# Four residual tiles and branch B's values, transposed as the rounded 32-bit type

## The chip, the core and the metric

One core of a Trainium2 chip runs the whole kernel. The time is device microseconds of one execution; the median of three runs is given. TensorE multiplies and also transposes 128x128 tiles (a matmul in transpose mode, with an identity matrix as second operand); VectorE and ScalarE do elementwise work; GpSimd (POOL) does small elementwise work and issues DMAs on its own queue; SyncE (SP) issues most of the other DMAs.

## The reference, cut to what matters

```
h = x + 1/2 * SwiGLU_1(RMSNorm(x))
u = RMSNorm(h)
[qA|kA|vA|qB|kB|vB|gA|gB] = u @ W_in
yA = NeighbourhoodAttention2D(qA, kA, vA)          # learned 2-D bias
yB = WindowedGQA(rope(qB), rope(kB), vB)           # learned sink logit
h = h + (sigmoid(gA) * (yA @ W_A) + sigmoid(gB) * (yB @ W_B)) @ W_out
h = h + 1/2 * SwiGLU_2(RMSNorm(h))
y = RMSNorm_final(h)
```

1024 tokens, width 1024, hidden width 2816, all in 32-bit floats.

## The kernel before

**Matmuls.** Every large product is done in three terms: an operand is split into a high part of the rounded 32-bit type (`F32R`) and a low part (`split`: ScalarE rounds to the high part, VectorE subtracts), and `mm3` issues high x high (L149), high x low (L153) and low x high (L155). Large products go through a Strassen scheme of seven products, P1 to P7, over 2x2 blocks (`products`); they need the blocks B11 and B21, made of the first four token tiles, and B22, T1, T2, T3 and T4, which also need the last four.

**Change of stage.** Between two parts of the layer the residual stream lies with tokens on the partitions, in eight tiles of 128 tokens (`res(t)`, tiles 0 to 3 in `fx`, 4 to 7 in `fa`); the next product needs it transposed. There are two such changes: from the first FFN to the input projection (`down1`, about 578 to 670 us), and from the attention's output to the second FFN (`down2`, about 1244 to 1296 us). `transition` runs them as a generator: for each tile, `pre` finishes it; `normed` squares it on ScalarE (L127), makes the factor on POOL (L130, L131) and scales it on VectorE into a buffer of the tag `xs` (L133); `turn_tile`, here `to_strassen`, transposes it with `turned` (8 transposes of 128x128 into two PSUM banks of the tag `d`, L142) and makes the Strassen blocks from the banks; `post` then drains ten steps of the early products, which fill TensorE between two tiles. The tag `xs` has two buffers, so tile t+1 is scaled while tile t waits to be turned. In the first change the tiles come in two halves of four. While tiles 4 to 7 go through, the top right block is kept in DRAM (`u_d`); for the last tile its copy is staged in the `xs` buffer that the tile itself lay in.

**Branch B's values.** `v_b` loads them (128 x 1024) from DRAM into an `xs` buffer, and `turn_v` transposes them with eight transposes (L1163).

**Order.** The first stage has an order written out by hand. In everything behind it a planner orders each engine's instructions at build time: it takes them in program order as priority, assumes a duration for each, and issues whichever is ready by its reckoning. Buffers of a tag are handed on when their last reader is done. `pin` keeps an instruction behind the one traced before it on its engine.

Other users of the identity `ident` are the warm-up transposes (`keep_busy`, L919), the spreading of statistics (L986) and the attention's probabilities (L1620).

The function `turned` is all of the transposing:

Of the kernel before, what the change touches and what calls it, by code (L numbers as in the profile page):

```python
# [9 lines left out]

F32 = mybir.dt.float32
# [20 lines left out]
def f32v(ap):  # L32
    return ap.bitcast(F32)
# [3 lines left out]
def trunk_kernel(ctx, tc, x, xt, n1, wg1, wu1, wd1, nm, win, rpb, sink, wa, wb, wout,  # L37
# [16 lines left out]
    def nm_(s):  # L54
        uid[0] += 1
        return f"{s}_{uid[0]}"

    ident = const.tile([P, P], F32, name="ident")
    make_identity(nc, ident)
    nhalf4 = const.tile([P, 4], F32, name="nhalf")  # L60
    nc.gpsimd.memset(nhalf4, -0.5)
    nhalf = nhalf4[:, 0:1]
# [72 lines left out]
        return xs  # L135

    def turned(xs):
        pts = []
        for half in range(2):
            pt = bank("d")  # L140
            for c in range(4):
                nc.tensor.transpose(pt[:, c * P:(c + 1) * P], xs[:, (half * 4 + c) * P:(half * 4 + c + 1) * P], ident)  # L142
            pts.append(pt.rearrange("p (c t) -> p c t", c=4))
        return pts

# [18 lines left out]

        return fx[t] if t < 4 else fa[:, (t - 4) * 1024:(t - 3) * 1024]

    def transition(pre, gain, turn_tile, post, halves=1, ahead=2):

        h, xs = {}, {}
        n = NTT // halves  # L170
        for base in range(0, NTT, n):
            for t in (base, base + 1):
                h[t] = pre(t)
            xs[base] = normed(h.pop(base), gain)
            yield
            for t in range(base, base + n):
                for k in range(t + 2, t + 1 + ahead) if base and t == base else (t + (ahead if base else 2),):
                    if k < base + n:
                        h[k] = pre(k)
                if t + 1 < base + n:  # L180
                    xs[t + 1] = normed(h.pop(t + 1), gain)
                turn_tile(t, xs.pop(t))
                if t:
                    post(t - 1)
                yield
        post(NTT - 1)
# [6 lines left out]

    kept = []

    def to_strassen(t, xs):

        pa, pb = turned(xs)
        tt = t % 4
        cols = slice(tt * P, (tt + 1) * P)  # L200

        def put(o, src, eng=None):
            h, l = rhs(o)
            split(h[:, :, cols], l[:, :, cols], src, eng)

        x11 = res(tt)[:, :512].rearrange("p (c t) -> p c t", c=4)
        x21 = res(tt)[:, 512:].rearrange("p (c t) -> p c t", c=4)
        if t < 4:
            put(B11, pa)
            put(B21, pb)  # L210
            nc.scalar.copy(x11, pa)
            nc.scalar.copy(x21, pb)
            return
        t1 = res(t)[:, :512].rearrange("p (c t) -> p c t", c=4)
        t2 = res(t)[:, 512:].rearrange("p (c t) -> p c t", c=4)
        nc.vector.tensor_tensor(t1, pa, x11, op=ALU.subtract)
        put(T1, t1)
        nc.vector.tensor_tensor(t2, pb, t1, op=ALU.subtract)
        put(T2, t2)
        put(B22, pb)  # L220
        nc.vector.tensor_tensor(x11, t2, x11, op=ALU.subtract)
        nc.vector.tensor_tensor(x21, x21, t2, op=ALU.subtract)
        if kept:
            x12 = xs[:, :512] if t == NTT - 1 else main.tile([P, 512], F32, tag="s1", bufs=1, name=nm_("s1"))
            nc.scalar.copy(x12.rearrange("p (c t) -> p c t", c=4), pa)
            nc.sync.dma_start(kept[0][t - 4], x12)

# [686 lines left out]
    def keep_busy(n):  # L914

        b = bank("g")
        for i in range(n):
            k = i % 4 * P
            nc.tensor.transpose(b[:, k:k + P], ident, ident)  # L919

    def first_stage():
        load, _, _, _, pieces, (multiply, finish), hand_over, load_early = hg
# [39 lines left out]
        def do(op, a):  # L962
# [3 lines left out]
            elif op == "add":  # L966
                d, e = [sq[k] for k in sums[int(a[0])]]
                nc.vector.tensor_tensor(d, d, e, op=ALU.add)
            elif op == "sum":
                i = int(a[0])  # L970
                if i == 0:
                    mean.append(bank("g"))
                for k in range(4):
                    nc.tensor.matmul(mean[0][:, k * P:(k + 1) * P], sq[3 * i][:, k * P:(k + 1) * P], ones, start=i + k == 0, stop=i == 1,
                                     skip_group_check=True)
            elif op == "eps":
                i = int(a[0])
                nc.vector.tensor_scalar(st[i][1], st[1][0] if i else mean[0].rearrange("p (k c) -> p k c", c=P)[:, :, 0], EPS, None, op0=ALU.add)
            elif op == "pow":
                i = int(a[0])  # L980
                nc.gpsimd.tensor_tensor(st[i][0], st[i][1], nhalf4, op=ALU.pow)
            elif op == "spread":
                i = int(a[0])
                r[i] = bank("d" if i else "g")
                for k in range(4):
                    nc.tensor.transpose(r[i][:, k * P:(k + 1) * P], st[i][0][:, k:k + 1].to_broadcast([P, P]), ident)  # L986
            elif op == "stat":
                t = int(a[0])
                nc.scalar.activation(toks[:, t - 4], toks[:, t - 4], AF.Square, scale=D ** -0.5,
                                     accum_out=st[1][0][:, t - 4:t - 3])  # L990
            elif op == "keep":
                rms["row"] = main.tile([P, 512], F32, tag="s1", bufs=1, name=nm_("s1"))
                nc.scalar.copy(rms["row"], r[0])
            elif a[0] == "X":
                c = int(a[1])
                h, l = [v[:, c, :] for v in rhs(B21)]
                if op == "hi":
                    nc.scalar.activation(h, block(c, 0, 1), AF.Copy, scale=n1c[:, 4 + c:5 + c])
                else:
                    nc.vector.scalar_tensor_tensor(out=l, in0=block(c, 0, 1), scalar=n1c[:, 4 + c:5 + c], in1=f32v(h),  # L1000
                                                   op0=ALU.mult, op1=ALU.subtract)
            elif op == "y":
                n, h, c = int(a[0][0]) - 1, int(a[0][1]) - 1, int(a[1])
                d, k = block(c, h, n), 4 * n + c
                nc.vector.scalar_tensor_tensor(out=d, in0=d, scalar=n1c[:, k:k + 1],
                                               in1=rms["row"] if (n, h) == (1, 0) else r[h], op0=ALU.mult, op1=ALU.mult)
            elif op == "t":
                c = int(a[1])
                y11, y21, y12, y22 = block(c, 0, 0), block(c, 0, 1), block(c, 1, 0), block(c, 1, 1)
                d, u, v = {"1": (y12, y12, y11), "2": (y22, y22, y12), "3": (y11, y22, y11), "4": (y21, y21, y22)}[a[0]]  # L1010
                nc.vector.tensor_tensor(d, u, v, op=ALU.subtract)
            elif a[0] in RIGHTS:
                c = int(a[1])
                src, g = block(c, *BLOCKS[a[0]]), RIGHTS[a[0]]
                if ar[g].dtype != F32R:
                    new_ar(g)
                h, l = [v[:, c, :] for v in rhs(RIGHTS[a[0]])]
                if op == "hi":
                    nc.scalar.copy(h, src)
                else:  # L1020
                    nc.vector.tensor_tensor(l, src, f32v(h), op=ALU.subtract)
            elif op == "load":
                i, m, half = [int(k) for k in a]
                load(i, m, half, {(0, 0): 4, (0, 1): 5, (1, 0): 6}[m, half])
            else:
                q = int(a[1]), a[0], int(a[2])
                if op == "mm":
                    if q not in mm:
                        mm[q] = multiply(*q)
                    drain(mm[q], 1)  # L1030
                elif op == "x":
                    drain(finish(*q), 1)
                else:
                    if q not in pc:
                        pc[q] = pieces(*q)
                    pc[q].pop(op)()
# [115 lines left out]

    def v_b():
        mix["vb"] = [new_fx(k, F32R).rearrange("p (t d) -> p t d", t=NTT) for k in (0, 1)]
        mix["vr"] = xs4()
        pin(nc.sync.dma_start(mix["vr"], z_d[17 * P:18 * P, :]))

    def turn_v():
        r = mix["vr"]
        for n in range(2):  # L1160
            pt = bank("g")
            for i in range(4):
                nc.tensor.transpose(pt[:, i * P:(i + 1) * P], r[:, (4 * n + i) * P:(4 * n + i + 1) * P], ident)  # L1163
            pt = pt.rearrange("p (b s d) -> p b s d", s=2, d=HD)
            for s in range(2):
                v = mix["vb"][s][:, 4 * n:4 * n + 4, :]
# [447 lines left out]
    def turn(un):  # L1614
        nk = un["nk"]
        un["p"] = [ws4()[:, :768].rearrange("p (k s t) -> p k s t", k=3, s=2) for _ in range(2)]
        for s in range(2):
            pt = bank("d")
            for i in range(nk):
                nc.tensor.transpose(pt[:, i * P:(i + 1) * P], un["pr"][s][:, i * P:(i + 1) * P], ident)  # L1620
            if len(un["v"]) == 2:
                dst = [un["p"][s][:, :nk, k, :] for k in range(2)]
            else:
# [317 lines left out]
```

## Time and profile before

| | |
|---|---|
| median of 3 runs | 1912.23 us (1911.99 to 1912.38) |
| the profiled execution | 1912.05 us, span of the profile 1910.1 us |
| instructions | 26150, of these 9020 matmuls or transposes |
| TensorE's granted clock, mean | 0.999 |
| DMA over the span | 192 GB/s |

The span runs from the first to the last instruction. An engine's busy time is the union of its instructions; matmuls overlap one another, so a row's duration is longer than the distance to the next start, and it is this distance that a matmul costs. PEld is TensorE's loading of weights, which overlaps. A transpose is shown as a MATMUL that reads `ident`. The type "f32" is shown for plain and rounded 32-bit operands of TensorE alike.

### The profile page before, as it was taken

The numbers are of one execution on the slowest core, as the hardware profiler recorded it, in microseconds if no ns is written. First come the engines' busy times: TensorE is split into PE (matmuls) and PEld (weight loads), VectorE is DVE, ScalarE is ACT, GpSimd is POOL, SyncE is SP. The second block draws the span as 40 slices with busy tenths as digits, with TensorE's granted clock in tenths as the row PEclk, the third lists the DMA queues.
The fourth block names the chain that finished last, engine by engine and source line by source line (L and its number), as shares of the span: only waits on it lengthen the run. The fifth ranks groups of instructions, "written<-read, shape, count | busy, mean of one in ns | idle before, by whom it ended". The sixth has DMA issues, their size and how long they took to land.

```text
span 1910.1 us, 26150 instructions
## 1 busy us (share of the span) xinstructions
PE 1901.1 (100%) x9020; PEld 1595.1 (84%) x9020; DVE 1456.1 (76%) x2644; ACT 961.3 (50%) x1876; POOL 244.3 (13%) x453
## 2 busy tenths in 40 slices
PE   9999999999999999999999999999999999999998
PEld 8888888888888888898898888888888888888886
DVE  8988888868957788666888999789665566559664
ACT  7533545544446543444898885274333333344453
POOL 0011232210000112211112300010010001000011
PEclk9999999999999999999999999999999999999999
DMA  7256977887454367855647969653333323492341
GB/s 270 95 188 217 336 273 289 298 293 282 127 166 135 112 206 225 243 192 206 181 123 207 296 227 335 232 195 132 136 111 107 108 89 111 162 357 93 110 139 61
DMA packets 176963, 365.84 MB, mean 192 GB/s; under 512 B 17728, under 2 KB 75968, under 8 KB 176832
## 3 DMA queue, kind: packets, MB, share of 16 engines
q1 hardware_dynamic: 136784, 236.23, 37.6%
q0 software_dynamic: 39184, 126.90, 19.2%
q8 instruction: 71, 1.16, 0.3%
q10 hardware_dynamic: 864, 1.05, 0.2%
q14 instruction: 60, 0.49, 0.1%
HBM read 244.06 MB, written 121.83 MB: 192 GB/s over the span
## 4 chain that ended last, share of the span: by engine, by line
PE 96%; ACT 2%; DVE 1%; DMA 0%; issue 0%; SPq 0%; POOLq 0%; POOL 0%; DVEq 0%
PE g L149 18%; PE g L155 18%; PE g L153 18%; PE d L155 12%; PE d L149 12%; PE d L153 12%; PE d L1620 2%; PE g L1634 1%; PE d L1596 1%; PE d L1597 1%; PE g L1639 1%; PE d L142 1%; ACT fa L1604 0%; ACT ws L95 0%; DMA fx<-in_xt_dram 0%; DVE ws L98 0%
## 5 line engine op out<-in xcount | busy, mean ns | idle before, releaser
L149 PE MATMUL g<-ar,ws 128*128 128x512 f32 x1062 | 407.0, 393 | 0.2
L153 PE MATMUL g<-ar,ws 128*128 128x512 f32 x1062 | 403.8, 390 | 0.0
L155 PE MATMUL g<-ar,ws 128*128 128x512 f32 x1062 | 402.6, 390 | 0.0
L149 PE MATMUL d<-ar,ws 128*128 128x512 f32 x706 | 275.3, 390 | 0.0
L155 PE MATMUL d<-ar,ws 128*128 128x512 f32 x706 | 274.9, 389 | 0.1
L153 PE MATMUL d<-ar,ws 128*128 128x512 f32 x706 | 274.8, 389 | 0.0
L155 PEld LDWEIGHTS g<-ar,ws 128*128 128x128 f32 x1062 | 199.2, 188 | 41.8
L153 PEld LDWEIGHTS g<-ar,ws 128*128 128x128 f32 x1062 | 199.4, 188 | 40.7
L149 PEld LDWEIGHTS g<-ar,ws 128*128 128x128 f32 x1062 | 196.4, 188 | 37.1 <-ACT xs L1331 1.1
L334 DVE TENSOR_TENSOR ws<-raw,ws 128x512 fp32r<-128x512 f32 x216 | 147.6, 689 | 78.5 <-ACT ws L327 77.7
L327 ACT CAST ws<-raw 128x512 fp32r<-128x512 f32 x216 | 132.7, 620 | 143.1 <-PE g L155 61.2
L155 PEld LDWEIGHTS d<-ar,ws 128*128 128x128 f32 x706 | 132.5, 188 | 28.0 <-DVE ws L334 0.5
L153 PEld LDWEIGHTS d<-ar,ws 128*128 128x128 f32 x706 | 132.6, 188 | 27.7 <-DVE ar L1000 0.3
L149 PEld LDWEIGHTS d<-ar,ws 128*128 128x128 f32 x706 | 132.7, 188 | 27.1
L95 ACT CAST ws<-raw 128x512 fp32r<-128x512 f32 x88 | 54.9, 623 | 115.5 <-PE d L155 63.6
L98 DVE TENSOR_TENSOR ws<-raw,ws 128x512 fp32r<-128x512 f32 x88 | 60.5, 688 | 55.2 <-ACT ws L95 55.1
L95 ACT CAST ar<-raw 128x512 fp32r<-128x512 f32 (+1 forms) x80 | 52.1, 654 | 84.4 <-PE g L153 51.5
L446 POOL DMA_DIRECT2D hid<-fx x91 | 49.5, 544 | 343.2 <-DVE fx L506 221.6
L149 PE MATMUL g<-ws,ws 128*128 128x512 f32 x232 | 90.9, 392 | 0.0
L153 PE MATMUL g<-ws,ws 128*128 128x512 f32 x232 | 90.3, 389 | 0.0
L155 PE MATMUL g<-ws,ws 128*128 128x512 f32 x232 | 90.1, 390 | 0.0
L95 ACT CAST ws<-ar 128x512 fp32r<-128x512 f32 x104 | 64.3, 618 | 47.4 <-PE g L155 25.4
(382 smaller groups left out, 3878.7 us busy)
## 6 DMA issues: line engine op xcount, KB each, us to landing
raw<-hid SPq DMA_DIRECT2D x70, 512.0 KB
hid<-fx POOLq DMA_DIRECT2D x91, 256.0 KB, 2.9
ar<-in_ffn_w_down_dram SPq DMA_DIRECT2D x32, 512.0 KB
raw<-in_ffn_w_up_dram SPq DMA_DIRECT2D x31, 512.0 KB
wo_d<-made POOLq DMA_DIRECT2D x28, 512.0 KB, 4.6
raw<-in_ffn_w_gate_dram SPq DMA_DIRECT2D x27, 512.0 KB
hid<-fa POOLq DMA_DIRECT2D x51, 256.0 KB, 2.9
ar<-zs_d POOLq DMA_DIRECT2D x48, 256.0 KB, 9.3
```

The lines of the kernel that those rows point to most:

```text
L95: hi = nc.scalar.copy(dst_hi, src)
L98: (eng or nc.vector).tensor_tensor(dst_lo, src, f32v(dst_hi), op=ALU.subtract)
L142: nc.tensor.transpose(pt[:, c * P:(c + 1) * P], xs[:, (half * 4 + c) * P:(half * 4 + c + 1) * P], ident)
L149: o = nc.tensor.matmul(b, lhs[0], r[0], start=first, stop=False, **kw)
L153: nc.tensor.matmul(b, lhs[0], r[1], start=False, stop=False, **kw)
L155: nc.tensor.matmul(b, lhs[1], r[0], start=False, stop=last, **kw)
L327: nc.scalar.copy(w[0][:, :512], a)
L334: nc.vector.tensor_tensor(w[0][:, 512:], a, f32v(w[0][:, :512]), op=ALU.subtract)
L446: nc.gpsimd.dma_start(hid[PRODUCTS.index(p), i], src)
L1596: nc.tensor.matmul(b[:, :nw], un["q"][s], un["kd"][s][:, k0 * P:k1 * P], start=True, stop=False)
L1597: nc.tensor.matmul(b[:, :nw], un["q"][s], un["kl"][s][:, k0 * P:k1 * P], start=False, stop=True)
L1620: nc.tensor.transpose(pt[:, i * P:(i + 1) * P], un["pr"][s][:, i * P:(i + 1) * P], ident)
```

## The change

The identity is made as a tile of the rounded type, and every other user reads it through a view as plain 32-bit float (`f32v`). In `transition`, for the tiles in `moved` (5 and 7, counted from 0, so the sixth and the eighth), the scaled tile is moved by a DMA on POOL's queue (512 KB, SBUF to SBUF, pinned in program order) into a second buffer of the tag `xs`, which has the rounded type; `turned` transposes that one with both operands and the result viewed as the rounded type. The bits are moved as they are. For the last tile of the first change of stage the staging of the top right block uses the buffer before the move (`spare`). Branch B's values are loaded into a tile declared with the rounded type and transposed as that type; the load is the same.

```
-    ident = const.tile([P, P], F32, name="ident")
-    make_identity(nc, ident)
+    ident = const.tile([P, P], F32R, name="ident")
+    nc.gpsimd.memset(f32v(ident), 0.0)
+    nc.gpsimd.affine_select(out=ident, in_=f32v(ident), compare_op=ALU.not_equal, fill=1.0, base=0, pattern=[[-1, P]],
+                            channel_multiplier=1)
...
     def turned(xs):
-        pts = []
+        i, pts = f32v(ident) if xs.dtype == F32 else ident, []
...
-                nc.tensor.transpose(pt[:, c * P:(c + 1) * P], xs[:, (half * 4 + c) * P:(half * 4 + c + 1) * P], ident)
+                nc.tensor.transpose(pt[:, c * P:(c + 1) * P].bitcast(xs.dtype), xs[:, (half * 4 + c) * P:(half * 4 + c + 1) * P], i)
...
-    def transition(pre, gain, turn_tile, post, halves=1, ahead=2):
+    def transition(pre, gain, turn_tile, post, halves=1, ahead=2, moved=(5, 7)):
...
+        def norm(t):
+            x = y = normed(h.pop(t), gain)
+            if t in moved:
+                x = main.tile([P, 1024], F32R, tag="xs", bufs=2, name=nm_("moved"))
+                pin(nc.gpsimd.dma_start(f32v(x), y))
+            xs[t] = x, y
...
-            xs[base] = normed(h.pop(base), gain)
+            norm(base)
...
-                    xs[t + 1] = normed(h.pop(t + 1), gain)
-                turn_tile(t, xs.pop(t))
+                    norm(t + 1)
+                turn_tile(t, *xs.pop(t))
...
-    def to_strassen(t, xs):
+    def to_strassen(t, xs, spare):
...
-            x12 = xs[:, :512] if t == NTT - 1 else main.tile([P, 512], F32, tag="s1", bufs=1, name=nm_("s1"))
+            x12 = spare[:, :512] if t == NTT - 1 else main.tile([P, 512], F32, tag="s1", bufs=1, name=nm_("s1"))
...
-        mix["vr"] = xs4()
-        pin(nc.sync.dma_start(mix["vr"], z_d[17 * P:18 * P, :]))
+        mix["vr"] = main.tile([P, 1024], F32R, tag="xs", bufs=2, name=nm_("vr"))
+        pin(nc.sync.dma_start(f32v(mix["vr"]), z_d[17 * P:18 * P, :]))
...
-                nc.tensor.transpose(pt[:, i * P:(i + 1) * P], r[:, (4 * n + i) * P:(4 * n + i + 1) * P], ident)
+                nc.tensor.transpose(pt[:, i * P:(i + 1) * P].bitcast(F32R), r[:, (4 * n + i) * P:(4 * n + i + 1) * P], ident)
```

The other lines of the diff replace `ident` by `f32v(ident)` where plain 32-bit data is transposed.

More of the change, by code (lines that the diff above doesn't have):

```diff
@@ L7 @@
 from concourse import mybir
-from concourse.masks import make_identity
 from concourse._compat import with_exitstack
@@ L918, in keep_busy @@
             k = i % 4 * P
-            nc.tensor.transpose(b[:, k:k + P], ident, ident)
+            nc.tensor.transpose(b[:, k:k + P], f32v(ident), f32v(ident))
     def first_stage():
@@ L985, in do @@
                 for k in range(4):
-                    nc.tensor.transpose(r[i][:, k * P:(k + 1) * P], st[i][0][:, k:k + 1].to_broadcast([P, P]), ident)
+                    nc.tensor.transpose(r[i][:, k * P:(k + 1) * P], st[i][0][:, k:k + 1].to_broadcast([P, P]), f32v(ident))
             elif op == "stat":
@@ L1619, in turn @@
             for i in range(nk):
-                nc.tensor.transpose(pt[:, i * P:(i + 1) * P], un["pr"][s][:, i * P:(i + 1) * P], ident)
+                nc.tensor.transpose(pt[:, i * P:(i + 1) * P], un["pr"][s][:, i * P:(i + 1) * P], f32v(ident))
             if len(un["v"]) == 2:
```

## The prediction

> **What bounds the kernel now.** I read the page first: busy shares, then the chain that ended last.
>
> ```profile
> span 1910.1 us, 26150 instructions
> ...
> PE 1901.1 (100%) x9020; PEld 1595.1 (84%) x9020; DVE 1456.1 (76%) x2644; ACT 961.3 (50%) x1876; POOL 244.3 (13%) x453
> ...
> PE 96%; ACT 2%; DVE 1%; DMA 0%; issue 0%; SPq 0%; POOLq 0%; POOL 0%; DVEq 0%
> ```
>
> TensorE carries 96% of the chain, so a matmul made shorter is worth its saving, and a wait put before a matmul costs its length, unless another engine takes the chain over. Hence two questions: how many TensorE slots does the change shorten and by how much, and do the four moved tiles still arrive before TensorE asks for them? The groups of line L142 (the turning of residual tiles) and L1163 (branch B's values) answer "how many".
>
> ```profile
> L142 PEld LDWEIGHTS d<-ident,xs x128: 137/140/144, 584.6 to 1294.5; 128*128 128x128 f32 x128
> L142 PE MATMUL d<-ident,xs x128: 270/272/299, 584.9 to 1294.6; 128*128 128x128 f32 x128
> ```
>
> ```profile
> L1163 PE MATMUL g<-ident,xs x8: 272/272/273, 811.0 to 811.7; 128*128 128x128 f32 x8
> ```
>
> 128 transposes are two changes of stage x 8 tiles x 8. Four of the sixteen tiles change type: 32 transposes, and 8 of L1163, 40 in all. The 272 ns are a latency; what counts is the slot, from TensorE's timeline around the sixth tile of the second change of stage.
>
> ```profile
> 1277.86 0.39 PE L155 MATMUL g<-ar,ws 128*128 128x512 f32 x1
> 1278.09 1.03 PE L142 MATMUL d<-ident,xs 128*128 128x128 f32 x8
> 1278.88 0.48 PE L149 MATMUL g<-ar,ws 128*128 128x512 f32 x1
> 1279.20 0.40 PE L153 MATMUL g<-ar,ws 128*128 128x512 f32 x1
> ```
>
> Eight starts cover 1.03 us, the last 0.272 long: (1.03 - 0.272)/7 = 108 ns from start to start. From 1278.09 to 1279.20 are eight transposes and one matmul of 512 columns (0.23): 0.88 us for eight, 110 ns each. There is no gap before or after, so the whole 0.88 is on the path.
>
> **The shortened slot.** No row shows a 128-column transpose of the rounded type. The matmuls of that type in this kernel have 256, 384 or 512 columns.
>
> ```profile
> 810.13 0.28 PE L155 MATMUL d<-ws,ar 128*128 128x256 f32 x1
> 810.25 0.28 PE L149 MATMUL d<-ws,ar 128*128 128x256 f32 x1
> ```
>
> ```profile
> 930.01 0.34 PE L1596 MATMUL d<-ar,ar 128*128 128x384 f32 x1
> 930.19 0.34 PE L1597 MATMUL d<-ar,ar 128*128 128x384 f32 x1
> ```
>
> 0.12, 0.18 and 0.23 us for 256, 384 and 512 columns: about 54 ns per 128 columns and 13 ns more, so 67 ns for 128 columns in one pass. The fp32 transpose, at 108 ns and 272 ns latency, looks like two passes (a 256-column matmul: 120 and 280). Is 108 perhaps one pass at half the clock, which no type would change? The start of the kernel answers.
>
> ```profile
> 1.52 6.23 PE L919 MATMUL g<-ident 128*128 128x128 f32 x28 [1.52 <-POOL ident masks.py:199]
> 7.41 0.59 PE L149 MATMUL d<-ar,ws 128*128 128x512 f32 x1
> 7.83 0.39 PE L153 MATMUL d<-ar,ws 128*128 128x512 f32 x1
> 8.06 0.40 PE L155 MATMUL d<-ar,ws 128*128 128x512 f32 x1
> ```
>
> There 28 of the same fp32 transposes fill 7.41 - 1.52 = 5.89 us, 210 ns each, and the first 512-column matmul behind them occupies 0.42 us where the next occupies 0.23. So TensorE ran at half speed there, the transposes with it, and 108 belongs to full speed: two passes. The Trainium skill (TensorE: Matmul & The Clock Gate, Part 4: PE-mode transpose) says that the full clock does not engage for transposes; by it 108 ns would be one pass at half clock, the change would shorten nothing and the time would stay at 1912.2. These rows speak against it for transposes between matmuls; the 28 at the start, which never sped up, fit it.
>
> The saving per slot is thus between 0 (something other than passes sets 108) and 108 - 54 = 54 ns; I take 108 - 67 = 41, from the slope of three measured widths. Per tile of eight 0.33 us; five groups give 1.64 us.
>
> **What of it is lost.** In the second change of stage VectorE is full, and the chain runs through it.
>
> ```profile
> 660.00:670.00 10.00, 10.00 (x49) 8.36 (x49) 10.00 (x18) 7.21 (x14) 0.54 (x1) 1.00 0.30 99
> 1270.00:1280.00 10.00, 10.00 (x54) 8.45 (x53) 10.00 (x16) 6.59 (x13) 0.87 (x2) 1.00 0.89 303
> 1280.00:1290.00 10.00, 10.00 (x50) 8.37 (x49) 10.00 (x17) 9.73 (x18) 1.43 (x3) 1.00 0.20 60
> ```
>
> ```profile
> 1292.15 0.61 DVE ws L334
> ...
> 1292.80 0.50 PE d L155
> ```
>
> (Columns of the first: stretch, then busy time of PE, PEld, DVE, ACT, POOL, granted clock, DMA share, GB/s.) At 1292.80 TensorE waits for VectorE's low half of a weight piece. The sixth tile of that stage (turned at 1278) only makes TensorE reach this wait 0.33 us sooner. So I count four groups: 4 x 0.33 = 1.3 us.
>
> **The moves.** Each moved tile adds one 512 KB DMA on POOL's queue and a second use of the two `xs` buffers. It has to wait for VectorE's scaling (L133) to write the source and for the turning of the tile before to free the other buffer. The rows of tiles 5 and 7 (counted from 0), first and second change of stage, VectorE:
>
> ```profile
> 640.37 1.28 DVE L133 SCALAR_TENSOR_TENSOR xs<-fa,st,gain 128x1024 f32<-128x1024 f32 x1 [2.24 <-POOL st L131]
> ...
> 658.35 1.28 DVE L133 SCALAR_TENSOR_TENSOR xs<-fa,st,gain 128x1024 f32<-128x1024 f32 x1
> ...
> 1269.25 1.29 DVE L133 SCALAR_TENSOR_TENSOR xs<-fa,st,gain 128x1024 f32<-128x1024 f32 x1 [0.17 <-POOL st L131]
> ...
> 1285.47 1.27 DVE L133 SCALAR_TENSOR_TENSOR xs<-fa,st,gain 128x1024 f32<-128x1024 f32 x1
> ```
>
> TensorE, tiles 4 to 7 of each:
>
> ```profile
> 639.91 1.03 PE L142 MATMUL d<-ident,xs 128*128 128x128 f32 x8
> 651.02 1.04 PE L142 MATMUL d<-ident,xs 128*128 128x128 f32 x8
> 656.02 1.03 PE L142 MATMUL d<-ident,xs 128*128 128x128 f32 x8
> 666.64 1.04 PE L142 MATMUL d<-ident,xs 128*128 128x128 f32 x8
> ...
> 1270.37 1.04 PE L142 MATMUL d<-ident,xs 128*128 128x128 f32 x8
> ...
> 1285.79 1.04 PE L142 MATMUL d<-ident,xs 128*128 128x128 f32 x8
> ...
> 1293.84 1.03 PE L142 MATMUL d<-ident,xs 128*128 128x128 f32 x8
> ```
>
> First change of stage: tile 5 is scaled at 641.65 and wanted at 651.02, 9.4 us; tile 7, 659.63 to 666.64, 7.0 us. Second: tile 5's move may start when tile 4 is turned (1271.41) and is wanted at 1278.09, 6.7 us; tile 7's when tile 6 is turned (1286.83), wanted at 1293.84, 7.0 us. The work that fills these 7 us is the early products, which need none of the last four tiles. How long does a POOL transfer take (columns: KB each, median us from issue to landing)?
>
> ```profile
> wo_d<-made POOLq DMA_DIRECT2D x28, 512.0 KB, 4.6
> ...
> ar<-zs_d POOLq DMA_DIRECT2D x48, 256.0 KB, 9.3
> ...
> zr_d<-xs POOLq DMA_DIRECT2D x5, 512.0 KB, 6.7
> ```
>
> 4.6 us from issue to landing is the commonest case of this size, 9.3 the slowest kind. I take 4.6: all four land with 2.1 us or more to spare, and cost TensorE nothing. At 9.3 TensorE would wait 2.6 us at 1278, 2.3 at 1294 and 2.3 at 667, 7.2 in all: that is the upper end. Below nothing is excluded, as a move gives no one anything earlier.
>
> Tile 6 then gets the buffer that tile 5's move reads, so its squares (ACT, at 1271.5 now) wait for the landing.
>
> ```profile
> 1271.50 1.06 ACT L127 ACTIVATE xs<-fa 128x1024 f32<-128x1024 f32 x1 [0.79 <-issue]
> ```
>
> 1271.4 + 4.6 = 1276.0 instead. Now VectorE's row for tile 6 ends 3.8 us after the squares began (1275.3); then at 1279.8, and it is turned at 1285.79: 6 us left. Behind the waiting squares on ACT stand casts of weight pieces; ACT has 3.4 of 10 us free there, and the planner of issue order may put the casts first. VectorE has other work queued to fill the place. I take nothing, with up to 2 us (the landing at 6.7 instead of 4.6) if it becomes a hole in VectorE's full stretch, which TensorE pays at 1292.8.
>
> Edits with one answer: the 0.5 us that each move occupies POOL's queue, and the store of hidden values that is behind the last one there, are covered by POOL's 13% load, and that store is read only in the second FFN's down part; the loads of w_down into `xs` blocks on SP's queue get their buffers some 4 us later, and these blocks are used only in the second FFN's down part; the gate loads behind them on SP may shift by as much, and their pieces are prepared several products ahead. Branch B's load is the same DMA under a view. The identity is made by the same two POOL instructions. Tiles 0 to 4 and 6, the attention's transposes and the warm-up use a view and cost the same.
>
> **Sum.** The profiled execution took 1912.05 us (span 1910.1, 1.95 around it), 0.18 below the median 1912.23. Minus 1.3: 1910.75 against it, 1910.9 against the median, -0.07%. What can be told from no change here is about 0.2%, 3.8 us.
>
> **The rivals.**
> - *No shorter slot, 1912.2.* The weight loads, not the passes, may set 108 ns. The timeline of loads shows two that wait for nothing at 0.11 us from each other:
>
> ```profile
> 585.63 0.19 PEld L149 LDWEIGHTS g<-ws,ws 128*128 128x128 f32 x1
> 585.74 0.19 PEld L153 LDWEIGHTS g<-ws,ws 128*128 128x128 f32 x1
> ```
>
>   If each load of 128 columns holds its port 0.11 us, a transpose with its own load cannot come oftener, whatever its type. For it: the equal number. Against: a transpose's load is 140 ns long and those are 188, so its port time may be shorter too. Price: gain 0, moves 0. The Trainium skill (TensorE: Matmul & The Clock Gate, LDWEIGHTS) gives columns / 1.2 ns, 107 for 128 columns; by it this rival holds and the time stays at 1912.2. The 0.11 row agrees with it.
> - *The moves land late, slower.* Place: tiles 5 and 7 of the second change of stage, where the DMA engines are 89% busy (1270 to 1280). It decides from a landing of 6.7 us on. At 9.3 us: 2.6 + 2.3 - 1.3 = +3.6, 1915.8; with the first change of stage late too, +5.9, 1918.1. Against: the DMA engines are at 20 to 30% in the stretches of the two tiles 7 (rows above).
> - *Other passes.* If the rounded type takes a slower path below 256 columns and a slot doubles, 40 x 110 ns = +4.4: 1916.6. No row speaks for it but that no such matmul is in the kernel.
> - *Another issue order.* After the first stage a planner orders the instructions; new due times may shift work far from the change. TensorE is full almost everywhere, so it can win little: 1907 to 1914.
>
> **How the numbers follow.** Forecast 0.47 (own range 1909.8 to 1911.6), no shorter slot 0.28, late moves 0.13, slower path 0.04, another order 0.08. Low end: five groups at 54 ns, 2.2, and a little luck of order: 1908.8. High end takes in the late moves in one stage: 1915.5. Faster by over 0.2% (below 1908.4) only by order: 0.06. Slower (above 1916.1): the slow path, the worst landings and bad order, 0.11. Within: 0.83.
>
> **What would show it.** Right: on the turning line, groups of eight starts in about 0.6 us for four tiles and L1163, 1.03 for the others; four moves on POOL's queue landing in 3 to 6.7 us; no wait of TensorE for them. Wrong: all groups still 1.03 (first rival); a TensorE gap before tile 5 or 7 of the second stage (second); a hole in VectorE between 1270 and 1292 with a longer stall at the low-half wait; or busy time moved in the attention, far from all of this.

## The result, and the profile after

| | before | changed |
|---|---|---|
| median | 1912.63 us (1911.99 to 1913.75, 7 runs) | 1921.46 us (1915.56 to 1926.23, 7 runs) |
| ratio to before | | 1.004, 95% interval 1.0025 to 1.0055 |
| the profiled execution | 1912.05 us, span 1910.1 | 1919.54 us, span 1917.7 |

Slower by 0.4%, where 1910.9 us was forecast. The changed kernel's executions lie further apart than those of the kernel before. The likely reason is the wait at 1100 us that is shown below: it has a different length from one profiled run to another, and the clock may fall behind it. A median here is one of such a mixture. Of the runs below, one execution of f2 (3206.9 us, mean clock 0.556) and one of the kernel before beside it (3899.87 us) were slow and are left out of every median.

The page of the changed kernel, busy time first:

```profile
span 1917.7 us, 26167 instructions
...
PE 1901.0 (99%) x9020; PEld 1593.0 (83%) x9020; DVE 1456.0 (76%) x2644; ACT 960.0 (50%) x1876; POOL 246.4 (13%) x457
```

TensorE is as busy as before (1901.0 us), and the span is 7.6 us longer: TensorE has gaps that it did not have. The turning line and branch B's values:

```profile
L143 PE MATMUL d<-ident,xs x96: 270/273/300, 585.3 to 1292.0; 128*128 128x128 f32 x96
...
L143 PE MATMUL d<-ident,moved x32: 223/247/258, 651.4 to 1300.9; 128*128 128x128 f32 x32
...
L1171 PE MATMUL g<-ident,vr x8: 223/248/252, 812.2 to 812.7; 128*128 128x128 f32 x8
```

The 40 transposes are there, and shorter: 247 ns instead of 273. TensorE's timeline at the places that matter (start, time, instruction; in brackets the wait before it), and three rows of the kernel before to hold against it:

```profile
640.34 1.03 PE L143 MATMUL d<-ident,xs 128*128 128x128 f32 x8
...
654.09 0.47 PE L150 MATMUL g<-ar,ws 128*128 128x512 f32 x1 [0.43 <-DVE fa L648]
...
659.51 0.50 PE L150 MATMUL g<-ar,ws 128*128 128x512 f32 x1 [0.38 <-DVE fa L1128]
668.06 0.79 PE L143 MATMUL d<-ident,moved 128*128 128x128 f32 x8
...
1100.02 0.34 PE L1604 MATMUL d<-ar 128*128 128x384 f32 x1
...
1103.91 0.44 PE L1604 MATMUL d<-ar 128*128 128x384 f32 x1 [3.38 <-DVE nmx L1609]
...
1282.57 0.80 PE L143 MATMUL d<-ident,moved 128*128 128x128 f32 x8
1283.20 0.46 PE L150 MATMUL g<-ar,ws 128*128 128x512 f32 x1
1283.50 0.39 PE L154 MATMUL g<-ar,ws 128*128 128x512 f32 x1
...
1288.36 0.47 PE L150 MATMUL g<-ar,ws 128*128 128x512 f32 x1 [0.84 <-ACT ar L96]
...
1300.27 0.85 PE L143 MATMUL d<-ident,moved 128*128 128x128 f32 x8 [1.78 <-DMA moved<-xs]
...
1303.10 0.39 PE L156 MATMUL d<-ar,ws 128*128 128x512 f32 x1
```

```profile
1099.04 0.34 PE L1596 MATMUL d<-ar 128*128 128x384 f32 x1
...
1099.39 0.34 PE L1596 MATMUL d<-ar 128*128 128x384 f32 x1
...
1295.86 0.39 PE L155 MATMUL d<-ar,ws 128*128 128x512 f32 x1
```

Each start against the same instruction before says how far the changed kernel is behind. At 640.34 it is 0.43 (the warm-up at half clock varies between executions; no moved tile has come yet); at 668.06, 1.42; at 1100.02, 0.98 (the last group of the first change of stage and branch B's values have given back 0.4); at 1103.91, 4.52; at 1282.57, 4.48; at 1303.10, 7.24. So the first change of stage cost 1.0, the attention 3.5, and the second change of stage 2.8, net of the shorter transposes.

**The attention.** TensorE waits for a row maximum (`nmx`), and VectorE, which makes it, is held one instruction earlier:

```profile
1099.17 0.07 DVE L1609 DVE_READ_ACCUMULATOR2_ANT nmx<- 128x1 f32 x1
1102.97 0.42 DVE L1572 TENSOR_TENSOR fa<-g,s 64x256 f32<-64x256 f32 x1 [3.72 <-DMA y_d<-fa]
```

L1572 writes branch A's values into rows 0 to 63 (the first four query blocks of a pair of heads) or 64 to 127 (the last four) of one buffer, and SP stores a half when it is full. From the code, this write is the first of the third pair, and what it overwrites is the half stored at 1083.61, not the one of 1096.64; the semaphore that it waits for is that of the store of 1083.61, too. SP's timeline:

```profile
1083.61 0.59 SPq L1574 DMA_DIRECT2D y_d<-fa  x1
...
1096.64 0.59 SPq L1574 DMA_DIRECT2D y_d<-fa  x1
```

That store, 256 KB, took 19.3 us to land (1102.87, by its semaphore in the trace). In the kernel before it was issued at 1082.63 and landed at 1097.94, after 15.3 us, and the same write went ahead at 1098.20 without a wait. So the kernel before had a margin of only 0.26 us here:

```profile
1082.63 0.59 SPq L1566 DMA_DIRECT2D y_d<-fa  x1
```

```profile
1098.20 0.41 DVE L1564 TENSOR_TENSOR fa<-g,s 64x256 f32<-64x256 f32 x1
```

The DMA engines are full there in the kernel before already (the last column but one is their share; it adds up the times of packets, so it can pass 1):

```profile
1095.00:1100.00 5.00, 5.00 (x35) 4.64 (x34) 4.63 (x17) 4.12 (x11) 2.31 (x4) 1.00 1.18 253
```

**The second change of stage.** Squares (ACT), scaling (DVE) and moves (POOL) of the last tiles, and the chain that ended last:

```profile
1282.01 1.07 ACT L128 ACTIVATE xs<-fa 128x1024 f32<-128x1024 f32 x1
...
1285.39 1.06 ACT L128 ACTIVATE xs<-fa 128x1024 f32<-128x1024 f32 x1
```

```profile
1280.66 0.69 DVE L99 TENSOR_TENSOR ar<-fa,ar 128x512 fp32r<-128x512 f32 x1 [0.88 <-ACT ar L96]
...
1284.53 1.28 DVE L134 SCALAR_TENSOR_TENSOR xs<-fa,st,gain 128x1024 f32<-128x1024 f32 x1 [0.77 <-POOL st L132]
...
1292.93 1.28 DVE L134 SCALAR_TENSOR_TENSOR xs<-fa,st,gain 128x1024 f32<-128x1024 f32 x1
```

```profile
1276.18 0.62 POOL L177 DMA_DIRECT2D moved<-xs  x1 [2.53 <-DVE ws L342]
...
1294.78 0.53 POOL L177 DMA_DIRECT2D moved<-xs  x1 [0.82 <-issue]
```

```profile
1292.33 0.69 DVE fa L514
1293.02 0.94 DVE xs L134
1293.96 0.80 issue
1294.78 5.36 DMA moved<-xs
1300.27 0.85 PE d L143 x8
```

All of this kernel is 4.48 us behind here. Less that, tile 5's move is issued at 1271.7, tile 6's squares start at 1277.5 (1271.5 before), 0.1 us after that move has landed (1281.93 in the trace), since it holds their buffer until then, tile 7's squares at 1280.9 (1280.1 before), its scaling at 1288.5 (1285.5 before), its move at 1290.3, and TensorE waits 1.78 us for it. The four moves' landing, from the rows of the tile `moved`:

```profile
DMA to landing us min/median/max: 3.2/4.7/5.8
```

One by one they are 4.0 and 3.2 us in the first change of stage, 5.8 and 5.4 in the second.

### The profile page after: what moved, and what is told of

It is laid out like the page before. It is cut to its first block, busy times and chain, and to the rows that moved or that the text cites. A ratio compares the mean times of both kernels' runs of the same rounds, so it can differ in the third digit from the quotient of the medians.

```text
span 1917.7 us, 26167 instructions
## 1 busy us (share of the span) xinstructions
PE 1901.0 (99%) x9020; PEld 1593.0 (83%) x9020; DVE 1456.0 (76%) x2644; ACT 960.0 (50%) x1876; POOL 246.4 (13%) x457
## 3 DMA queue, kind: packets, MB, share of 16 engines
q1 hardware_dynamic: 136784, 236.23, 37.4%
## 5 line engine op out<-in xcount | busy, mean ns | idle before, releaser
L342 DVE TENSOR_TENSOR ws<-raw,ws 128x512 fp32r<-128x512 f32 x216 | 147.9, 689 | 77.5 <-ACT ws L335 76.6
```

Of the source, the lines that this page charges most:

```text
L342: nc.vector.tensor_tensor(w[0][:, 512:], a, f32v(w[0][:, :512]), op=ALU.subtract)
```

## The experiments

Diffs are against the changed kernel, or, where the text says so, against the kernel before. Each time is compared with the kernel before on the same chip.

**One change of stage at a time; the moves without the type; the transfers without the type.**

```
-merge.into(transition(down2, gain, to_strassen, behind(hg), 2, 3), hg)
+merge.into(transition(down2, gain, to_strassen, behind(hg), 2, 3, moved=()), hg)             # e1: none in the second
-down.into(transition(down1, gain, to_strassen, behind(pg, (0, 1)), 2), pg)
+down.into(transition(down1, gain, to_strassen, behind(pg, (0, 1)), 2, moved=()), pg)         # e2: none in the first
-    x = main.tile([P, 1024], F32R, tag="xs", bufs=2, name=nm_("moved"))
+    x = main.tile([P, 1024], F32, tag="xs", bufs=2, name=nm_("moved"))                       # e3: moves, no rounded type
-    pin(nc.gpsimd.dma_start(f32v(x), y))
+    pin(nc.gpsimd.dma_start(spare_d, y))                                                     # e4: a store that nobody reads
```

> Moves only in the first change of stage, branch B's values as before. Theory A (the attention: the two extra transfers of the first change shift POOL's queue, and the store of y lands late at about 1100 us, 3.5 us and more of waiting): +4 to +12 us against before, with a TensorE wait of 3 us or more at the scores (L1604) in the profile and unequal times from run to run. Theory B (waits at the changes of stage alone): first change +1.3 us of waits less 0.5 us of shorter slots, +1 us, no wait at the scores.

> Moves only in the second change of stage, branch B's values as before. Theory A: no wait in the attention (it lies ahead of these moves), only the waits at 1283 to 1303 us, +1.5 to +2.5 us, times as even as those of before. Theory B: the same +1.5 to +2.5 us, as the larger part of the loss.

> All four moves, but every transpose (branch B's values too) stays plain 32-bit. What the type gains is lost, 40 slots x 29 ns = 1.2 us: theory A and B both expect the changed kernel's time plus about 1.2 us and the same waits. If instead the time is that of before, the type of the transposes and not the moves is what costs.

> No move: the four tiles are stored by POOL's queue into a DRAM tile that nobody reads, the transposes read the plain tile as before. The same four transfers of 512 KB on the same queue, but no second xs buffer and no wait for the landing. Theory A (queue and traffic): waits in the attention remain, +3 to +10 us and uneven. Theory B (waits for moved tiles and buffers): within 0.5 us of before.

In all four branch B's values are transposed plain, in e4 the tiles too. The kernel before took 1912.53 us beside them. e1: 1916.24, ratio 1.0015 (1.0006 to 1.0024). e2: 1915.9, 1.0016 (1.0007 to 1.0025). e3: 1918.3, 1.0033 (1.002 to 1.0046). e4: 1914.47, 1.0012 (1.0004 to 1.0021). The wait at 1100 us is there with the moves of the first change of stage (e1, 2.7 us) and with mere stores (e4, 2.8 us); it is absent in e2, which has instead the waits of the second change of stage. e3 has both (1.3 and 1.6 us), and no gain from the type. So there are two separate costs, and neither needs the type. Several sizes were missed: e1 came out 0.3 us under its range, e2 0.9 us above it, e4 between its two theories, and e3, expected 1.2 us above the changed kernel, lost 3 us less than it.

e2 also shows why a gap costs more than its length. Its windows (columns as in the prediction) and TensorE's timeline:

```profile
1292.00:1296.00 4.00, 2.39 (x15) 1.75 (x13) 4.00 (x8) 3.96 (x9) 0.00 (x0) 1.00 0.51 177
1296.00:1300.00 4.00, 4.00 (x16) 3.18 (x15) 4.00 (x8) 2.68 (x5) 0.00 (x0) 0.62 0.74 243
1300.00:1304.00 4.00, 4.00 (x18) 3.32 (x17) 4.00 (x7) 0.93 (x2) 0.55 (x1) 0.96 0.75 282
```

```profile
1295.53 0.84 PE L143 MATMUL d<-ident,moved 128*128 128x128 f32 x8 [1.61 <-DMA moved<-xs]
...
1296.99 0.63 PE L156 MATMUL d<-ar,ws 128*128 128x512 f32 x1
1297.42 0.63 PE L150 MATMUL d<-ar,ws 128*128 128x512 f32 x1
```

After a wait of 1.61 us the granted clock is 0.62 over 4 us, and a 512-column matmul takes 0.43 us of TensorE instead of 0.23. In the changed kernel's profiled execution no such fall follows the waits of 3.38 and 1.78 us. This is part of the spread of its times: its mean clock was 0.999 in the executions of 1915.56 to 1919.54 us and 0.996 in those above 1925, and 0.003 of 1920 us is about 6 us.

**Is it the bytes, or the mere fact of more transfers?** f1 puts two stores of 512 bytes into the kernel before, where the two moves would be; f2 adds six to the changed kernel; f3 and f4 have no transfer added ahead of the attention.

```
-    pin(nc.gpsimd.dma_start(f32v(x), y))
+    pin(nc.gpsimd.dma_start(spare_d[0:1, 0:P], y[0:1, 0:P]))       # f1, first change only
+    for _ in range(3):                                             # f2, first change only, behind the move
+        pin(nc.gpsimd.dma_start(spare_d[0:1, 0:P], y[0:1, 0:P]))
+... moved=()) in both changes                                      # f3, branch B's values rounded
+... moved=()) in the first, moved=(7,)) in the second              # f4, branch B's values plain
```

> The kernel before with one thing added: in the first change of stage POOL stores 512 bytes of tile 5 and of tile 7 into DRAM that nothing reads. Theory 'place in the list': POOL numbers its transfers round eight semaphores. Two more transfers shift these numbers by two, and with them the place that one wait has in the list of waits of POOL's load raw<-y_d in the attention (about 1042 us). The wait that ends last, for the store y_d<-xs, moves from the last place to one with two more pairs of waits behind it, and POOL issues the load about 0.5 us after SP's three transfers instead of together with them. So with 1 KB of added traffic: the first load lands 7.5 to 8 us after its issue instead of 5.3, the later transfers run 1 to 3 us late, VectorE's write of branch A's values waits for y_d<-fa at about 1100 us, TensorE waits 2.5 to 3.5 us there, and the time is 1914.5 to 1916.5. Theory 'traffic or time' (the bytes of the moved tiles, or the shift in time that their waits cause, disturb the attention): 1 KB and no waits do nothing, no wait there, within 0.5 us of the kernel before.

> The changed kernel with six stores of 512 bytes added behind the two moves of the first change of stage (three behind each), so that POOL has issued eight more transfers than in the kernel before, and the numbers are back where they were. 'Place in the list': POOL's load raw<-y_d is issued within 0.1 us of SP's transfers again, TensorE's wait at about 1100 us is gone or under 0.5 us, and what is left are the waits of the two changes of stage less the gain of the type: 1915.5 to 1918, 3 to 5 us less than the changed kernel. 'Traffic or time': the wait stays at 2.5 us or more, and the time is that of the changed kernel, 1919 to 1923, or some tenths above it for the six issues.

> Only branch B's values are transposed as the rounded type; no tile is moved. Both theories: eight slots of 79 ns instead of 108, 0.23 us; the group of L1171 in 0.80 us; 1912.2 to 1912.5 where the kernel before has 1912.5, not to be told apart in time. My first forecast had 0.33 us for this group.

> Only tile 7 of the second change of stage is moved and transposed as the rounded type. Theory 'two moves on one pair of buffers': tile 7 came late because the move of tile 5 held a buffer until it landed, which put the squares and the scaling of tile 6, and with them all of tile 7, later. With tile 5's move gone, tile 7 is scaled at about 1286.8, its move is issued at about 1287 and lands at about 1292.4, before TensorE asks at 1293.8: no wait of TensorE for it, no step at 1283, 1912 to 1913.2. Theory 'one move is too slow here': the move lands 7 us or more after its issue and TensorE waits 1 us or more at 1294, with a clock drop behind it, 1914 to 1916.

Before 1912.74. f1: 1915.34, 1.0008 (1.0 to 1.0017). f2: 1921.05, 1.005 (1.0037 to 1.0063). f3: 1912.36, 1.0 (0.9991 to 1.0008). f4: 1912.99, 0.9996 (0.9988 to 1.0005). One kilobyte seems enough: in f1, six of eleven executions lie between 1915.3 and 1918.4, where the kernel before has four of 28 above 1915.3; but the interval of its ratio still touches 1 (h1 below is clear). In its profiled one (1912.68) the wait is short:

```profile
DVE fa L1573 <- DMA y_d<-fa: 1.0, 1, 1.0
```

The start of its transfers at 1042 us fits the "place in the list": POOL's load is issued 0.5 us behind SP's first transfer (1042.27 against 1041.79), where the kernel before has 1041.86 against 1041.85. But f2, with the load again next to SP's transfers, keeps the wait (2.4 us of TensorE) and its time. So the list is not the cause, at least not alone.

f4 closes the half of the second change of stage:

```profile
1287.46 0.62 POOL L177 DMA_DIRECT2D moved<-xs  x1 [5.15 <-PE d L143]
```

```profile
1293.98 0.79 PE L143 MATMUL d<-ident,moved 128*128 128x128 f32 x8
```

One move alone is issued when tile 6 is turned, lands in 4.9 us and costs nothing that can be told, just as the prediction had it for this tile.

**Does distance cure it?** g1 to g4 write and store branch A's values in quarters, so that a place is written again six units of the attention behind its store instead of four.

```
-  both = y[j // 4 * HD:j // 4 * HD + HD].rearrange("p (s t) -> p s t", s=2)
+  k = j % 4 // 2 * 512
+  both = y[j // 4 * HD:j // 4 * HD + HD, k:k + 512].rearrange("p (s t) -> p s t", s=2)
...
-  if j in (3, 7):
+  if j % 2:
```

g1 is this edit in the changed kernel, g2 in the kernel before, g3 in one with branch B's values and tile 7 of the second change of stage alone, g4 in the changed kernel with `moved=(7,)` in the second.

> The changed kernel, with branch A's values in the attention written and stored in quarters of 64 x 512 instead of halves of 64 x 1024, in the same place and of the same total size: twelve stores of 128 KB for six of 256 KB. A piece is written again 6 units of the attention after its store was issued instead of 4, some 20 us instead of 14. Theory 'no margin': the store that is issued at 1083.6 and lands 19.3 us later costs the changed kernel all of the wait at 1100 us, because VectorE writes the same place again 14 us later; with 6 units of distance the wait is gone whatever made the store late, and so is the drop of the clock behind it: 1914.5 to 1917, 4 to 6 us less than the changed kernel, and the slowest runs come nearer to the fastest. Rival 'the load on the DMA engines itself': TensorE waits for another transfer there instead (POOL's loads ar<-zs_d or fx<-v_d, late as well), 1919 to 1922.

> The same quarters in the kernel before; nothing else. 'No margin': the kernel before stands at the edge there (its profiled execution doesn't wait; some of its runs are 2 to 4 us above the others): the median stays within 0.7 us, 1912 to 1912.8, and the runs above 1914.5 are fewer. Rival: the six more stores cost something of their own, 1913 to 1915.

> What the earlier runs point to: branch B's values and tile 7 of the second change of stage alone as the rounded type, no other move, and the quarters. Two groups of 0.23 us: 1911.7 to 1912.4, and no runs above 1914.5. If the quarters cost something, as in their own run.

> The changed kernel with the quarters, and without the move of tile 5 in the second change of stage: tiles 5 and 7 of the first and 7 of the second are moved. 'Two moves on one pair of buffers': with tile 5's move gone the second change of stage costs nothing (step at 1283 and wait at 1294 gone), and 'no margin' takes away the wait of the attention; what is left is the first change of stage, +0.54 and +0.8 by the changed kernel's profile, less four groups of 0.23 us: 1912.5 to 1913.5. Rival: 1 us or more in the second change of stage or in the attention, 1914 to 1917.

Before 1913.19. g1: 1918.23, 1.0025 (1.0014 to 1.0035). g2: 1912.97, 0.9997 (0.9988 to 1.0005). g3: 1912.5, 0.9997 (0.9989 to 1.0006). g4: 1913.28, 1.0002 (0.9993 to 1.001). In g4 no loss is left that can be told, and it still has three of the four moves and all of branch B's values. g1 missed its range by 1.2 us. Its waits of TensorE:

```profile
PE g L150 <- DVE s L1568: 1.6, 1, 1.6
PE d L143 <- DMA moved<-xs: 1.6, 1, 1.6
```

The wait for `y_d<-fa` is gone, but a smaller one has taken its place some 10 us later (in g4 it is there as 2.0 us for `ws<-wb_d`, weights that come late): other transfers are late besides that store, and the distance takes away about half of the wait. The distance and the size of a store change together here; no run separates them. g3 is the fastest here, but not to be told apart from the kernel before.

**What makes the transfers late?** h1 has eight small stores instead of f1's two, so that POOL's numbering round eight semaphores, and with it the lists of waits in the attention, are those of the kernel before; h2 issues the moves on SP's queue; h3 moves tile 5 of the second change alone. i1 has two POOL memsets in place of f1's stores, i2 eight small stores at 1 us, i3 is h1 with the quarters.

```
-    pin(nc.gpsimd.dma_start(f32v(x), y))
+    for _ in range(4):                                             # h1 and i3, first change only
+        pin(nc.gpsimd.dma_start(spare_d[0:1, 0:P], y[0:1, 0:P]))
+    pin(nc.sync.dma_start(f32v(x), y))                             # h2
+... moved=()) in the first, moved=(5,)) in the second              # h3, branch B's values plain
+    pin(nc.gpsimd.memset(spare_s, 0.0))                            # i1, first change only
     nc.gpsimd.memset(ones, 1.0)
+    for _ in range(8):                                             # i2, no move
+        nc.gpsimd.dma_start(spare_d[0:1, 0:P], f32v(ident)[0:1, :])
```

> The kernel before with eight stores of 512 bytes on POOL's queue in the first change of stage (four behind tile 5's scaling, four behind tile 7's). POOL's transfers are numbered round eight semaphores, so that from there on the numbers, and the places in every list of waits, are those of the kernel before, unlike with two tiny stores. 'Place in the list': POOL's load raw<-y_d at 1042 us is issued with SP's transfers (within 0.1 us), lands in 5.3 to 5.6 us, nothing waits in the attention, and the median is that of the kernel before, within 0.7 us, with few runs above 1914.5. 'Any transfer put on POOL's queue' (whatever it is that additional transfers leave behind there): the loads of 1042 to 1051 us run 1 us late as with two tiny stores and the median is 1.5 to 3 us above the kernel before.

> The changed kernel with the four moves issued by SP instead of POOL; POOL's transfers are those of the kernel before. Theory 'POOL's queue' (list of waits or other): the attention runs as before, no wait of TensorE at 1100 us, and what is left are the waits of the two changes of stage and, new, whatever stands behind the moves on SP's queue: 1914.5 to 1918, 3 to 6 us under the changed kernel. Rival 'the moves themselves' (the shift of everything behind by 1 us, the bytes): the wait at 1100 us stays at 2.5 us or more, 1919 to 1923.

> Only tile 5 of the second change of stage is moved and transposed as the rounded type. Theory 'two moves on one pair of buffers': the move of tile 5 holds its buffer until it lands, so that the squares and the scaling of tile 6 come later and TensorE loses about 0.8 us at 1283 us, 0.3 us in two steps behind it; tile 7 needs no move and is turned without a wait for a transfer. Less 0.17 for the type: about +0.9 us, 1913 to 1914.2. Rival: the delay is made up before tile 7, 1912.2 to 1913.

> The kernel before with two POOL memsets of one element per partition in the first change of stage, where other runs have two stores of 512 bytes; no transfer is added. Theory 'transfers leave something behind': no wait in the attention, median within 0.7 us of the kernel before, at most 2 of 11 runs above 1914.5. Rival 'more instructions on POOL': as with the two tiny stores, half of the runs above 1914.5, median 1.5 to 3 us above.

> The kernel before with eight stores of 512 bytes on POOL's queue at 1 us, where POOL is idle until 15.9 us; the numbers round the eight semaphores are in step. 'Something left behind': as with eight at 650 us, the median 3 to 5 us above the kernel before, most runs above 1914.5. Rival 'near in time' (what the stores at 650 us shift in the projection right behind them goes on to the attention): no change, within 0.7 us.

> Eight stores of 512 bytes in the first change of stage, as before, and branch A's values in quarters, so that a place is written again 6 units behind its store instead of 4. 'No margin': the transfers of 1042 to 1051 us run 1 us late as without the quarters, but VectorE no longer waits for y_d<-fa; the median falls from +4.2 us to within 1.2 us of the kernel before. Rival: another late transfer takes the wait's place, +2 us or more.

Before 1912.86 for h, 1912.41 for i. h1: 1917.08, 1.0017 (1.0008 to 1.0027), 4.2 us more for 4 KB, though its load is issued together with SP's transfer (1041.60 and 1041.59): the list of waits is out. h2: 1920.96, 1.0037 (1.0024 to 1.005), with VectorE's wait as long as in the changed kernel:

```profile
  DMA y_d<-fa: 3.7, 1
```

So it is not POOL's queue either. i1: 1912.78, 1.0001 (0.9992 to 1.001): instructions without a transfer do nothing. i3: 1913.09, 1.0002 (0.9993 to 1.0011): the same eight stores as in h1 cost nothing that can be told once the place is written again later. They still make transfers late there: the slowest of POOL's loads described below takes 14.6 us in i3, and 13.0 in g2, which has the quarters alone. h3: 1914.27, 1.0005 (0.9996 to 1.0013), just above its range; TensorE's waits in the second change of stage are there though tile 7 is not moved:

```profile
PE g L150 <- ACT ar L96: 0.6, 1, 0.6
PE d L156 <- DVE ws L342: 0.6, 1, 0.6
```

i2 missed by far for another reason, 1935.65, 1.0116 (1.0102 to 1.013): the eight stores go to one place, each waits for the one before, and POOL makes the first stage's factor only at 37.4 us.

```profile
PE g L997 <- POOL st L992: 20.2, 1, 20.2
```

TensorE is 23.2 us late at 21 us and 23.05 us late at the end, and nothing waits in the attention: 1935.65 - 23.1 = 1912.6. Transfers added at the start thus leave nothing behind; added at about 650 us they do. The slowest of POOL's four loads from `y_d`, issued from 1041.86 us on, lands after 14.5 us in the kernel before (the view gives no landing of SP's transfers, so the store of 1082.63 is not in it):

```profile
DMA to landing us min/median/max: 5.3/9.7/14.5
```

It is 13.6 to 14.5 in e2, f3, f4, h3, i1 and (23 us later) i2, and 15.3 to 16.3 in e1, e3, e4, f1, f2, h1, h2 and the changed kernel.

The traces say more than this view: they have sixteen rises of each transfer's semaphore, and the last rise is the landing. For the store of 1083.61 the fifteenth came after 15.9 us and the last after 19.3; for the same store of the kernel before, after 14.2 and 15.3. For the slowest load the fifteenth came after 13.1 us in both kernels, the last after 16.3 in the changed one and 14.5 before. For all transfers issued between 1040 and 1070 us, the last rise came on average 2.1 us behind the fifteenth in the changed kernel, 1.3 to 2.2 in e1, e3, f1, f2, h1 and h2, 0.8 in the kernel before and 0.4 to 0.7 in e2, f3, f4, h3, i1 and (23 us later) i2. Only e4 doesn't fit (0.8; there the fifteenth rise of the slowest load is late as well, after 14.7 us). So what is late is for the most part one of sixteen parts, and not the transfers as a whole; which part it is, the traces don't tell. What of the added transfers is carried over these 390 us stays open; a shift in time does not explain it (f1's starts are 0.26 us earlier than before, the changed kernel's 1 us later), nor do the bytes, the list, or the queue.

## Why the prediction was wrong

- **What bounds the kernel** held: TensorE's path, and every wait put before it costs its length, or more where the clock falls.
- **Forty slots** held. **The shortened slot** had the right mechanism and the wrong size. The row at 1282.57 gives (0.80 - 0.247)/7 = 79 ns from start to start, not 67. From 1282.57 to 1283.50 are eight transposes and one matmul of 0.23: 0.70 us for eight, where it was 0.88, a saving of 0.18 per group and 0.9 us in five, not 0.33 and 1.3 in four. The step that failed is the slope of 256 to 512 columns drawn down to 128: it priced the passes alone, and no row of before showed whether a slot that short leaves room for its own load. That the load is what adds the 12 ns is not shown. The Trainium skill (TensorE: Matmul & The Clock Gate, Back-to-back issue gap) gives about 81 ns a matmul for a stream of loads and matmuls of 128 columns. The 79 ns agree with it; an estimate of this term by it would have been (108 - 81) x 8, 0.22 per group.
- **The rival "no shorter slot"** fell: slots of 79 ns, each with a load of its own, are there, and the granted clock around them is 1.00 (1280 to 1290). With it fell the two rules of the Trainium skill (TensorE: Matmul & The Clock Gate) that were weighed. The 79 ns are less than the 107 that its section LDWEIGHTS gives a load, and transposes between matmuls do run at the full clock, unlike what its Part 4: PE-mode transpose says.
- **The moves land in 4.6 us**: that size was right in the median (4.7), but in the second change of stage, where it counted, they took 5.8 and 5.4. The start of tile 5's move was right (1271.7 against 1271.4, less the 4.48 us); tile 6's squares came 1.5 us later than the 1276.0 of the working, most of it by this longer landing.
- **"all four land with 2.1 us or more to spare"** failed at tile 7 of the second change of stage. The working put tile 6 later and left tile 7 where it was, scaled at 1285.47 and moved from 1286.83. It was scaled at 1288.5 and moved from 1290.3. Its factor was ready, but its scaling stands in VectorE's queue behind tile 5's block sums, and these behind tile 6's late scaling: twelve instructions of about 0.6 us between the two scalings (1284.53 and 1292.93), without a gap. About 1.8 of the 3.0 us come from this; the other 1.2 are two instructions (L342, L514) that the planner now puts in front of tile 7's scaling. **"I take nothing, with up to 2 us"** is the term: 2.8 net. The hole in VectorE that the prediction named as its condition is there (0.88 and 0.77 us, at 1280.66 and 1284.53; the kernel before has none in that stretch). h3 shows 1.4 us in the median with tile 5's move alone, though its interval touches 1; f4 shows none with tile 7's alone; and g4, which is g1 without tile 5's move, is 1918.23 - 1913.28 = 5 us faster, any fall of the clock included.
- **The first change of stage** was taken as free by the 9.4 and 7.0 us of slack of the moved tiles; these were turned without a wait for their moves. But there too tile 6 came later: its squares start at 646.89 (642.37 before), 0.3 us after tile 5's move has landed, and VectorE idles 1.34 us before its scaling. TensorE then waits for VectorE, 0.43 and 0.38 us: 1.0 net by the starts.
- **The queue effects, "covered by POOL's 13% load",** were put at nothing; this is the step that cost most, 3.5 us. It asked whether POOL's queue has room, not who, hundreds of microseconds later, depends on when a transfer lands. The DMA engines' share around 1100 us (1.18), not POOL's, was the row to read: the half written again at 1098.20 had been stored only 15.6 us earlier and had landed 0.26 us before, and in f3 the same write already waited 0.2 us. The prediction named "busy time moved in the attention, far from all of this" as a sign of error, but gave it no price. Why transfers added at 650 us make those at 1040 to 1100 us late stays open.
- **The sums** hold but one: the high end, 1915.5, is said to take in late moves in one stage, which the working had put at 1915.8.
- **The rivals.** "Late moves" was the right mechanism in the right stage for part of the loss, by another route than a landing of 9.3 us. "Other passes" is out, since the slots became shorter. "Another issue order" is out for the attention: the order on ScalarE, VectorE, POOL and SP is that of before from 820 to 1270 us; only the timing moved. In the second change of stage it did happen, as said above for tile 7, and it lost time.

## What to carry to other kernels

Before adding a transfer, look for buffers that are written again soon after a store in stretches where the DMA engines are full: their margin, from issue to the next write against the time to landing, was 0.26 us here, so that 4 KB of other transfers cost 4 us. A longer distance took this cost away in i3 though its origin had not been found. Where two buffers are handed round, a move holds the source until it lands, so the work on the next tile to use that buffer comes late; follow it to its end, through every engine that it queues on. In the second change of stage, moving tile 7 alone cost nothing that can be told (f4).

## What had not been expected of the hardware

- Eight stores of 512 bytes at about 650 us raise the median by 4.2 us (h1), two by 2.6 us (f1, not clear of noise), with a wait at 1100 us in both profiles; two memsets in their place do nothing (1912.78 against 1912.41).
- A 256 KB store took 19.3 us to land where the DMA engines were full, 3.4 of them for the last of its sixteen parts, while 512 KB from buffer to buffer took 5.36 us elsewhere.
- A gap of 1.61 us was followed by a granted clock of 0.62 over 4 us in one execution, and gaps of 3.38 and 1.78 us by none in another. (At 1104 to 1108 us the clock is 0.64 to 0.66 behind the wait in e4, f2 and h2, and 1.00 in e1 and e3.) The Trainium skill (TensorE: Matmul & The Clock Gate, Why this matters for your kernels) asks for no gap above about 3 us; here the shorter gap had the fall and the longer had none.
